# Gated linear attention: a pair's two heads in the partition halves, one tile per direction, and the states made behind both heads' masked products

## The chip, the cores and the metric

The kernel runs on one core of a Trainium2 chip. The metric is the device time of one execution in microseconds (us). The engines named below are TensorE (PE; its weight loads are PEld), VectorE (DVE), ScalarE (ACT), GpSimd (POOL) and SyncE (SP, which issues the DMAs). Each engine works through its own queue in order and waits on semaphores.

## The reference

Two layers over 256 latent tokens and 256 context tokens, width 1024: a SwiGLU half step, a token mixer, a second half step. The mixer has three branches (latent attention, pooling, gated linear attention), each projected, gated and summed. The change is in the third one. It has four heads with a key width of 64 and a value width of 128, in chunks of 64 tokens, one scan forwards and one backwards over context and latent tokens; for each direction:

```
b = jnp.cumsum(ac, axis=3)                       # log decay within a chunk
b_last = b[:, :, :, -1:, :]
q_t, k_t, k_end = qc * exp(b), kc * exp(-b), kc * exp(b_last - b)
A = where(tril, einsum("bhnik,bhnjk->bhnij", q_t, k_t), 0.0)
o_intra = einsum("bhnij,bhnjv->bhniv", A, vc)
dS = einsum("bhnjk,bhnjv->nbhkv", k_end, vc)
decay = exp(b_last)
S_next = decay[..., None] * S + dS               # scan over the chunks
o = o_intra + einsum("bhnik,bhnkv->bhniv", q_t, S)
```

The two directions' outputs are added, normalized per head and token (RMS), and multiplied by a gate.

## The kernel before, in words

The 512 tokens (latent ones first) are the free axis, features are the partitions. Weights come by DMA into raw tiles and are split into a rounded part `whi` (ACT) and a rest `wlo` (DVE, L197); a dense product is three matmuls, at L219, L220 and L221. Most of the kernel is such products.

`mixer` runs generators side by side. In layer 0 `attend` and then `gla` run as one chain; in layer 1, where queries and outputs are the 256 latent tokens only (`n` is 256), they alternate. After each step of a chain, a table of credits (`FILL`) says how much of `filler` is emitted: dense products of other branches whose matmuls (`fill`, `ps`) stand between the steps on TensorE. A list scheduler then fixes each engine's order; what it made of it is shown below.

`gla` takes the heads in two pairs per layer. For a pair, `gla_prepare` makes both directions' logits, decays and sums. `la` is k_end (L1175), turned token-major by transposes (L1189) into `ket`. `qt` and `kt` are q_t and k_t: one tile per head, with direction 0 in partitions 0 to 63 and direction 1 in 64 to 127; since the sources `gq`, `gk` and `e` hold the pair's heads in partition halves, this takes six VectorE instructions of 64 partitions per direction (L1182 to L1184, the last for the decays `dec`).

`gla_pair` then takes one head after the other: 16 small products `ds` (L1210, 64 tokens by 64 key columns, 128 value columns), 14 state steps on VectorE (L1222 and L1224, 64 partitions by 128), the products `A` (L1231), two masked copies (L1232) and their sum `Asum` (L1237); after a step of `filler`, the output `o`: A times values (L1244) and query times state (L1246), where one matmul has both directions in its 128 rows; the first chunk of each direction has a zero state that GpSimd sets (L1212, L1213). Square, sum, Ln, Exp and a product (L1255) normalize it, and it is transposed back (`ot`, L1259).

Of the kernel before, what the change touches and what calls it, by code (L numbers as in the profile page):

```python
# [12 lines left out]
ALU = mybir.AluOpType  # L13
AX = mybir.AxisListType

P = 128
# [121 lines left out]
class Net:  # L138
# [1002 lines left out]
    def gla_prepare(self, c, ready):  # L1141


        nc, l, n = self.nc, self.l, self.n
        cst, vec = self.cst, self.vec[l]
        rst = cst[:, C_RST:C_RST + T]
        gq, gk = self.gq[c], self.gk[c]
        chunk = lambda t: t.rearrange("p (n c) -> p n c", c=64)
# [9 lines left out]
        for d, ps in enumerate(logits):  # L1158
# [20 lines left out]
            o = slice(d * 64, d * 64 + 64)  # L1179
            for hh in range(2):  # L1180
                r = slice(hh * 64, hh * 64 + 64)
                nc.vector.scalar_tensor_tensor(out=qt[hh][o, 0:n], in0=gq[r, 0:n], scalar=0.125, in1=e[r, 0:n], op0=ALU.mult, op1=ALU.mult)  # L1182
                nc.vector.tensor_tensor(out=kt[hh][o, 0:n], in0=gk[r, 0:n], in1=b[r, 0:n], op=ALU.mult)
                nc.vector.tensor_copy(dec[o, hh, :], chunk(e)[r, :, end])  # L1184
# [11 lines left out]
    def gla_pair(self, c, qt, kt, ket, dec):  # L1196

        nc, l, n = self.nc, self.l, self.n
        cst, vec, gv = self.cst, self.vec[l], self.gv
        for hh in range(2):  # L1200
            h = 2 * c + hh
            hv = slice(h * P, (h + 1) * P)

            st = [self.slot(name="st").rearrange("p (n v) -> p n v", n=4) for _ in range(2)]
            dst = [self.ps("ds").rearrange("p (n v) -> p n v", n=4) for _ in range(2)]
            for ch in range(8):
                tt, par = ch // 2, ch % 2
                r = slice(par * 64, par * 64 + 64)
                for d in range(2):
                    nc.tensor.matmul(dst[par][d * 64:d * 64 + 64, tt, :], ket[d][r, tt * P + hh * 64:tt * P + hh * 64 + 64],  # L1210
                                     gv[tt][r, hv], start=True, stop=True)
            nc.gpsimd.memset(st[1][0:64, 0, :], 0.0)  # L1212
            nc.gpsimd.memset(st[1][64:128, 3, :], 0.0)  # L1213
            order = [[4, 5, 6, 7, 0, 1, 2, 3], [7, 6, 5, 4, 3, 2, 1, 0]]
            for i in range(7):
                for d in range(2):
                    o = slice(d * 64, d * 64 + 64)
                    x, y = order[d][i], order[d][i + 1]
                    ds = dst[x % 2][o, x // 2, :]
                    to = st[y // 4][o, y % 4, :]  # L1220
                    if i == 0:
# [168 lines left out]
```

## Time and profile before

| | us |
|---|---|
| Time, median of 3 runs | 2170.09 (2168.61 to 2172.72) |
| Time of the profiled execution | 2169.75 |
| Its span, first to last instruction | 2167.9 |
| TensorE busy | 2081.1 (96% of the span) |
| VectorE busy | 1483.3 (68%) |
| ScalarE busy | 881.2 (41%) |
| Mean granted TensorE clock | 0.984 of full speed |

A busy share is a mean over stages. Matmuls overlap one another in the pipeline, so their durations are longer than the distance from one start to the next; it is the distance that counts for a stretch of them. The time minus the span (1.85 us) is what lies around the profiled instructions.

### The profile page before, as it was taken

To read this page: it belongs to the slowest core of one execution; us is meant where nothing else is said; L and a number is where in the kernel's file an instruction comes from. 1 tells how busy PE (TensorE), PEld (TensorE's weight loads), DVE (VectorE), ACT (ScalarE), POOL (GpSimd) and SP (SyncE) were. 2 spreads that over 40 slices of the span, in tenths; PEclk is the share of its full clock that TensorE was granted. 3 is DMA by queue.
4 is the path that set the end of the run, shared out by engine and by line. 5 is a ranking of instruction groups with operands and counts; after the bars stand their busy time and mean duration, and the time that the engine had idled before them with its cause. 6 is when DMAs were issued, how large, how long until landed. Compare 5 with 4: busy or idle time off the path is not lost.

```text
span 2167.9 us, 29909 instructions
## 1 busy us (share of the span) xinstructions
PE 2081.1 (96%) x11340; PEld 1749.1 (81%) x11340; DVE 1483.3 (68%) x2950; ACT 881.2 (41%) x1797; POOL 5.2 (0%) x26
## 2 busy tenths in 40 slices
PE   7999999898999989999999989999999978999999
PEld 4888878776777778888888888888888867898997
DVE  4577777867686775666876785667554788666564
ACT  5322232445345445433223243223343546565552
POOL 0000000000000000000000000000000000000000
PEclk9999999999999999999999999999999989999999
DMA  9355554514442223445555444456451333466663
GB/s 315 100 157 154 176 166 139 139 55 120 113 112 59 78 65 93 125 121 153 168 169 149 143 138 118 144 145 176 128 139 42 89 90 96 122 172 185 185 194 128
DMA packets 431072, 290.44 MB, mean 134 GB/s; under 512 B 16464, under 2 KB 386768, under 8 KB 430928
## 3 DMA queue, kind: packets, MB, share of 16 engines
q1 hardware_dynamic: 430016, 287.09, 46.0%
q8 instruction: 89, 1.46, 0.3%
q10 hardware_dynamic: 912, 1.44, 0.2%
q14 instruction: 55, 0.45, 0.1%
HBM read 287.44 MB, written 1.05 MB: 133 GB/s over the span
## 4 chain that ended last, share of the span: by engine, by line
PE 72%; DVE 13%; DMA 9%; ACT 4%; issue 2%; ACTq 0%; SPq 0%; DVEq 0%
PE ps L219 17%; PE ps L220 17%; PE ps L221 17%; DMA raw<-in_ffn_w_dram 8%; PE fill L219 4%; DVE wlo L197 4%; PE fill L221 4%; PE fill L220 4%; DVE adaacc L358 2%; ACT whi L185 2%; DVE st L1224 2%; PE sc L1031 1%; PE av L1067 1%; PE pt L1049 1%; PE ada L327 1%
## 5 line engine op out<-in xcount | busy, mean ns | idle before, releaser
L197 DVE TENSOR_TENSOR wlo<-raw,whi 128x512 fp32r<-128x512 f32 (+3 forms) x912 | 531.4, 619 | 290.2 <-ACT whi L185 282.4
L185 ACT ACTIVATE whi<-raw 128x512 fp32r<-128x512 f32 (+3 forms) x912 | 472.2, 568 | 521.7 <-DMA raw<-in_ffn_w_dram 472.5
L219 PE MATMUL ps<-uhi,whi 128*128 128x512 f32 (+1 forms) x1620 | 565.3, 351 | 8.1 <-ACT uhi L185 5.1
L221 PE MATMUL ps<-uhi,wlo 128*128 128x512 f32 (+1 forms) x1620 | 563.2, 348 | 1.0 <-DVE wlo L197 0.9
L220 PE MATMUL ps<-ulo,whi 128*128 128x512 f32 (+1 forms) x1620 | 563.8, 348 | 0.0
L219 PEld LDWEIGHTS ps<-uhi,whi 128*128 128x128 f32 x1620 | 309.1, 192 | 52.7 <-ACT uhi L185 8.3
L221 PEld LDWEIGHTS ps<-uhi,wlo 128*128 128x128 f32 x1620 | 310.1, 191 | 41.0 <-DVE wlo L197 3.0
L220 PEld LDWEIGHTS ps<-ulo,whi 128*128 128x128 f32 x1620 | 310.3, 192 | 38.1 <-DVE ulo L475 0.8
L358 DVE SCALAR_TENSOR_TENSOR adaacc<-raw,csil,adaacc 128x512 f32<-128x512 f32 x420 | 294.6, 744 | 1.0 <-DMA raw<-in_w_ada_dram 0.2
L219 PE MATMUL ps<-hi,whi 128*128 128x512 f32 (+1 forms) x738 | 271.4, 369 | 8.0 <-DVE h L501 6.6
L221 PE MATMUL ps<-hi,wlo 128*128 128x512 f32 (+1 forms) x738 | 270.6, 367 | 0.0
L220 PE MATMUL ps<-lo,whi 128*128 128x512 f32 (+1 forms) x738 | 270.4, 367 | 0.0
L219 PE MATMUL fill<-uhi,whi 128*128 128x512 f32 (+1 forms) x576 | 204.7, 355 | 0.0
L221 PE MATMUL fill<-uhi,wlo 128*128 128x512 f32 (+1 forms) x576 | 196.6, 341 | 0.0
L220 PE MATMUL fill<-ulo,whi 128*128 128x512 f32 (+1 forms) x576 | 196.3, 341 | 0.0
L219 PEld LDWEIGHTS ps<-hi,whi 128*128 128x128 f32 x738 | 139.8, 190 | 30.8 <-DVE h L501 7.0
L221 PEld LDWEIGHTS ps<-hi,wlo 128*128 128x128 f32 x738 | 140.0, 190 | 22.6
L220 PEld LDWEIGHTS ps<-lo,whi 128*128 128x128 f32 x738 | 140.0, 190 | 22.5 <-DVE lo L197 0.2
L570 DVE TENSOR_TENSOR silu<-silu,ps 128x512 f32<-128x512 f32 (+1 forms) x88 | 54.2, 616 | 131.2 <-ACT silu L185 79.9
L219 PEld LDWEIGHTS fill<-uhi,whi 128*128 128x128 f32 x576 | 110.0, 191 | 21.9 <-issue 10.3
L185 ACT ACTIVATE silu<-ps 128x512 f32<-128x512 f32 (+1 forms) x88 | 47.4, 538 | 194.5 <-PE ps L221 194.5
L220 PEld LDWEIGHTS fill<-ulo,whi 128*128 128x128 f32 x576 | 110.1, 191 | 13.7 <-issue 2.6
(267 smaller groups left out, 2215.8 us busy)
## 6 DMA issues: line engine op xcount, KB each, us to landing
raw<-in_ffn_w_dram SPq DMA_DIRECT2D x198, 512.0 KB, 4.4
raw<-in_w_ada_dram SPq DMA_DIRECT2D x128, 512.0 KB, 3.8
raw<-in_w_in_dram SPq DMA_DIRECT2D x86, 512.0 KB, 4.4
raw<-in_ffn_w_dram SPq DMA_DIRECT2D x48, 384.0 KB, 4.1
raw<-in_ffn_w_dram SPq DMA_DIRECT2D x48, 320.0 KB, 3.2
raw<-in_w_branch_dram SPq DMA_DIRECT2D x48, 256.0 KB, 2.8
ada<-in_w_ada_dram SPq DMA_DIRECT2D x32, 256.0 KB, 5.4
raw<-in_w_out_dram SPq DMA_DIRECT2D x16, 512.0 KB, 4.9
```

Of the source, the lines that this page charges most:

```text
L185: i = self.nc.scalar.activation(**k)
L197: self.nc.vector.tensor_tensor(out=lo, in0=src, in1=f32hi, op=ALU.subtract)
L219: mm(out, wh, xh, start=start, stop=False)
L220: mm(out, wh, xl, start=False, stop=False)
L221: mm(out, wl, xh, start=False, stop=stop)
L327: nc.tensor.matmul(ps[32 * g:32 * g + 32, :], self.csil[:, k, :], r[i], start=(k < 4), stop=(k >= 4))
L358: nc.vector.scalar_tensor_tensor(out=acc[s], in0=r[i], scalar=c, in1=acc[s], op0=ALU.mult, op1=ALU.add)
L570: nc.vector.tensor_tensor(out=s[:, 0:n], in0=s[:, 0:n], in1=p3[:, 0:n], op=ALU.mult)
L1031: nc.tensor.matmul(sc[:, 0:nk], q[h][:, tt * P:(tt + 1) * P], keys[h][:, k0:T], start=True, stop=True)
L1049: nc.tensor.transpose(pt[:, (2 * x + j) * P:(2 * x + j + 1) * P], ps_[j][:, (kt + x) * P:(kt + x + 1) * P], self.ident)
L1067: nc.tensor.matmul(av[0][64 * x:64 * x + 64, s * NL:(s + 1) * NL], v[2 * s + kt][:, (h + x) * 64:(h + x) * 64 + 64], pts[x][kt // 2][:, (k ...
L1224: nc.vector.scalar_tensor_tensor(out=to, in0=st[x // 4][o, x % 4, :], scalar=dec[o, hh, x:x + 1], in1=ds, op0=ALU.mult, op1=ALU.add)
```

## The change

`qt`, `kt` and `dec` now have one tile per direction, with the pair's two heads in the partition halves, so three VectorE instructions of 128 partitions per direction make them. `gla_pair` first makes the products A, the masks and the sums of both heads, then, after a step of `filler`, for each direction the `ds` products of both heads (seven chunks, not eight: the last chunk's product was never used) and seven state steps of 128 partitions that serve both heads. The outputs follow head by head: one matmul for each chunk and direction, with 64 rows, without those whose state is zero; the GpSimd memsets are gone. The transposes of both heads come at the end. The number of steps (yields) of the generator is the same, and so is the amount of `filler` between pairs.

```diff
--- before.py
+++ after.py
@@ -1176,12 +1176,9 @@
             ket.append(la)
             self.act(out=e, in_=b, func=AF.Exp, scale=1.0 / 16)
             self.act(out=b[:, 0:n], in_=b[:, 0:n], func=AF.Exp, scale=-1.0 / 16)
-            o = slice(d * 64, d * 64 + 64)
-            for hh in range(2):
-                r = slice(hh * 64, hh * 64 + 64)
-                nc.vector.scalar_tensor_tensor(out=qt[hh][o, 0:n], in0=gq[r, 0:n], scalar=0.125, in1=e[r, 0:n], op0=ALU.mult, op1=ALU.mult)
-                nc.vector.tensor_tensor(out=kt[hh][o, 0:n], in0=gk[r, 0:n], in1=b[r, 0:n], op=ALU.mult)
-                nc.vector.tensor_copy(dec[o, hh, :], chunk(e)[r, :, end])
+            nc.vector.scalar_tensor_tensor(out=qt[d][:, 0:n], in0=gq[:, 0:n], scalar=0.125, in1=e[:, 0:n], op0=ALU.mult, op1=ALU.mult)
+            nc.vector.tensor_tensor(out=kt[d][:, 0:n], in0=gk[:, 0:n], in1=b[:, 0:n], op=ALU.mult)
+            nc.vector.tensor_copy(dec[:, d, :], chunk(e)[:, :, end])
             yield "g1"
         for d in range(2):
             pt = self.ps("ket")
@@ -1197,54 +1194,60 @@
 
         nc, l, n = self.nc, self.l, self.n
         cst, vec, gv = self.cst, self.vec[l], self.gv
+        nt = n // P
+        order = [[4, 5, 6, 7, 0, 1, 2, 3], [7, 6, 5, 4, 3, 2, 1, 0]]
+        hvs = [slice((2 * c + hh) * P, (2 * c + hh + 1) * P) for hh in range(2)]
+        As = []
         for hh in range(2):
-            h = 2 * c + hh
-            hv = slice(h * P, (h + 1) * P)
-
-            st = [self.slot(name="st").rearrange("p (n v) -> p n v", n=4) for _ in range(2)]
-            dst = [self.ps("ds").rearrange("p (n v) -> p n v", n=4) for _ in range(2)]
-            for ch in range(8):
-                tt, par = ch // 2, ch % 2
-                r = slice(par * 64, par * 64 + 64)
-                for d in range(2):
-                    nc.tensor.matmul(dst[par][d * 64:d * 64 + 64, tt, :], ket[d][r, tt * P + hh * 64:tt * P + hh * 64 + 64],
-                                     gv[tt][r, hv], start=True, stop=True)
-            nc.gpsimd.memset(st[1][0:64, 0, :], 0.0)
-            nc.gpsimd.memset(st[1][64:128, 3, :], 0.0)
-            order = [[4, 5, 6, 7, 0, 1, 2, 3], [7, 6, 5, 4, 3, 2, 1, 0]]
-            for i in range(7):
-                for d in range(2):
-                    o = slice(d * 64, d * 64 + 64)
-                    x, y = order[d][i], order[d][i + 1]
-                    ds = dst[x % 2][o, x // 2, :]
-                    to = st[y // 4][o, y % 4, :]
-                    if i == 0:
-                        nc.vector.tensor_copy(to, ds)
-                    else:
-                        nc.vector.scalar_tensor_tensor(out=to, in0=st[x // 4][o, x % 4, :], scalar=dec[o, hh, x:x + 1], in1=ds,
-                                                       op0=ALU.mult, op1=ALU.add)
+            o = slice(hh * 64, hh * 64 + 64)
             for d in range(2):
-                o = slice(d * 64, d * 64 + 64)
                 ps = self.ps("A")
-                for tt in range(n // P):
+                for tt in range(nt):
                     t = slice(tt * P, (tt + 1) * P)
-                    nc.tensor.matmul(ps[:, t], kt[hh][o, t], qt[hh][o, t], start=True, stop=True)
+                    nc.tensor.matmul(ps[:, t], kt[d][o, t], qt[d][o, t], start=True, stop=True)
                 nc.vector.copy_predicated(
                     out=self.amask[d][:, 0:n].rearrange("p (t i) -> p t i", i=P),
-                    mask=self.msk[:, d:d + 1, :].to_broadcast([P, n // P, P]),
+                    mask=self.msk[:, d:d + 1, :].to_broadcast([P, nt, P]),
                     data=ps[:, 0:n].rearrange("p (t i) -> p t i", i=P))
             A = self.slot(name="Asum")
             nc.vector.tensor_tensor(out=A[:, 0:n], in0=self.amask[0][:, 0:n], in1=self.amask[1][:, 0:n], op=ALU.add)
-            yield "g3"
-
+            As.append(A)
+        yield "g3"
+
+        sts = []
+        for d in range(2):
+            st = [self.slot(name="st").rearrange("p (n v) -> p n v", n=4) for _ in range(2)]
+            dst = [self.ps("ds").rearrange("p (n v) -> p n v", n=4) for _ in range(2)]
+            for x in order[d][0:7]:
+                tt, par = divmod(x, 2)
+                r = slice(par * 64, par * 64 + 64)
+                for hh in range(2):
+                    nc.tensor.matmul(dst[par][hh * 64:hh * 64 + 64, tt, :], ket[d][r, tt * P + hh * 64:tt * P + hh * 64 + 64],
+                                     gv[tt][r, hvs[hh]], start=True, stop=True)
+            for i in range(7):
+                x, y = order[d][i], order[d][i + 1]
+                ds, to = dst[x % 2][:, x // 2, :], st[y // 4][:, y % 4, :]
+                if i == 0:
+                    nc.vector.tensor_copy(to, ds)
+                else:
+                    nc.vector.scalar_tensor_tensor(out=to, in0=st[x // 4][:, x % 4, :], scalar=dec[:, d, x:x + 1], in1=ds,
+                                                   op0=ALU.mult, op1=ALU.add)
+            sts.append(st)
+        yield "g3"
+        sqs = []
+        for hh in range(2):
+
+            hv, A, o = hvs[hh], As[hh], slice(hh * 64, hh * 64 + 64)
             po = self.ps("o")
-            nt = n // P
             for tt in range(nt):
                 t = slice(tt * P, (tt + 1) * P)
                 nc.tensor.matmul(po[:, t], A[:, t], gv[tt][:, hv], start=(tt == 0), stop=False)
             for ch in range(2 * nt):
-                nc.tensor.matmul(po[(ch % 2) * 64:(ch % 2) * 64 + 64, (ch // 2) * P:(ch // 2 + 1) * P], qt[hh][:, ch * 64:ch * 64 + 64],
-                                 st[ch // 4][:, ch % 4, :], start=False, stop=(ch >= 2 * nt - 2))
+                for d in range(2):
+                    if ch != order[d][0]:
+                        nc.tensor.matmul(po[(ch % 2) * 64:(ch % 2) * 64 + 64, (ch // 2) * P:(ch // 2 + 1) * P],
+                                         qt[d][o, ch * 64:ch * 64 + 64], sts[d][ch // 4][o, ch % 4, :],
+                                         start=False, stop=(ch >= 2 * nt - 2 and d == (0 if ch == 7 else 1)))
             sq = self.slot(name="sqo")
             self.act(out=sq[:, 0:n], in_=po[:, 0:n], func=AF.Square)
             rstd = self.tiny(8, "orstd")
@@ -1253,7 +1256,9 @@
             self.act(out=rstd[:, 4:4 + nt], in_=rstd[:, 0:nt], func=AF.Ln, scale=1.0 / P, bias=self.eps[:, 0:1])
             self.act(out=rstd[:, 4:4 + nt], in_=rstd[:, 4:4 + nt], func=AF.Exp, scale=-0.5)
             nc.vector.tensor_tensor(out=by_tile(sq), in0=by_tile(po), in1=rstd[:, 4:4 + nt].unsqueeze(2).to_broadcast([P, nt, P]), op=ALU.mult)
+            sqs.append(sq)
             yield "g4"
+        for sq in sqs:
             pt = self.ps("ot")
             for tt in range(nt):
                 nc.tensor.transpose(pt[:, tt * P:(tt + 1) * P], sq[:, tt * P:(tt + 1) * P], self.ident)
```

What it does to the order. On TensorE, layer 0, first pair: before, from the first head's `ds` to its transposes (`ps` and `fill` rows between are left out and counted in the text behind).

```order
L1210 MATMUL ds<-gv,ket 64x128 x16
L1231 MATMUL A<-qt,kt 128x128 x8
L219 MATMUL ps<-hi,whi 128x512
...
L1244 MATMUL o<-gv,Asum 128x128 x4
L1246 MATMUL o<-st,qt 64x128 x8
L219 MATMUL fill<-uhi,whi 128x512
...
L1259 MATMUL ot<-cst_72,sqo 128x128 x4
```

The same engine and place after the change, for both heads.

```order
L1207 MATMUL A<-qt,kt 128x128 x16
...
L1225 MATMUL ds<-gv,ket 64x128 x28
...
L1244 MATMUL o<-gv,Asum 128x128 x4
L1248 MATMUL o<-st,qt 64x128
L219 MATMUL fill<-uhi,whi 128x512
L220 MATMUL fill<-ulo,whi 128x512
L1248 MATMUL o<-st,qt 64x128 x13
...
L1244 MATMUL o<-gv,Asum 128x128 x4
L1248 MATMUL o<-st,qt 64x128 x14
...
L1264 MATMUL ot<-cst_72,sqo 128x128 x8
```

Before, 24 `ps` matmuls stand between A and `o` of the first head and 21 `fill` matmuls for the second. Now 24 `ps` matmuls stand between A and `ds`, and 12 `fill` matmuls between `ds` and the first `o`; 22 more come before the second `o`. In the second pair of layer 0 it was 21 and 9 between A and `o`, and is now 12 between A and `ds`, 24 between `ds` and `o`, and 12 between the two outputs.

On VectorE, the same place, before (one head).

```order
L796 TENSOR_TENSOR gate<-gate 128x512
L1222 COPY st<-ds 64x128 x2
L1224 SCALAR_TENSOR_TENSOR st<-st,dec,ds 64x128 x12
L1232 COPY_PREDICATED amask_181<-msk,A 128x512
L1232 COPY_PREDICATED amask_182<-msk,A 128x512
L794 TENSOR_TENSOR gate<-gate,ps 128x512
L1237 TENSOR_TENSOR Asum<-amask_181,amask_182 128x512
```

And after (both heads; seven rows of dense work, L197, L794 and L796, are left out between).

```order
L1213 TENSOR_TENSOR Asum<-amask_181,amask_182 128x512
L1208 COPY_PREDICATED amask_181<-msk,A 128x512
L1208 COPY_PREDICATED amask_182<-msk,A 128x512
L1213 TENSOR_TENSOR Asum<-amask_181,amask_182 128x512
...
L1231 COPY st<-ds 128x128
L1233 SCALAR_TENSOR_TENSOR st<-st,dec,ds 128x128 x3
L1231 COPY st<-ds 128x128
L1233 SCALAR_TENSOR_TENSOR st<-st,dec,ds 128x128 x8
L197 TENSOR_TENSOR wlo<-raw,whi 128x512
L1233 SCALAR_TENSOR_TENSOR st<-st,dec,ds 128x128
```

The mask sums no longer stand behind the states; the states now end last, and one run of 14 serves both heads where there were two runs.

On TensorE, layer 1, first pair, after the change (`sc` are attention scores, `pool` the pooling branch's product, `rq` a transpose for the attention).

```order
L1225 MATMUL ds<-gv,ket 64x128 x23
L1017 MATMUL rq<-cst_72,rq 128x128 x2
L1031 MATMUL sc<-k,q 128x512 x2
L1244 MATMUL o<-gv,Asum 128x128 x2
L1248 MATMUL o<-st,qt 64x128
L219 MATMUL pool<-hilo,whi 128x256
L1244 MATMUL o<-gv,Asum 128x128 x2
L1248 MATMUL o<-st,qt 64x128
L220 MATMUL pool<-hilo,whi 128x256
L221 MATMUL pool<-hilo,wlo 128x256
L1248 MATMUL o<-st,qt 64x128 x14
```

Before, the first head's `o` stood ahead of `rq` and `sc`, and the second head's `ds`, A and `o` behind them. Now both heads' last 14 output matmuls stand together behind the first scores.

## Rows read from the trace of the kernel before

**Rows 1.** The page's first part: busy time and share of the span, first engines.
```profile
PE 2081.1 (96%) x11340; PEld 1749.1 (81%) x11340; DVE 1483.3 (68%) x2950; ACT 881.2 (41%) x1797; POOL 5.2 (0%) x26
```

**Rows 2.** Windows: us; busy PE, PEld, DVE, ACT, POOL; granted TensorE clock; DMA.
```profile
690.00:820.00 130.00, 119.45 (x725) 95.42 (x724) 95.15 (x176) 65.41 (x114) 1.59 (x8) 0.99 0.24 65
...
1740.00:1790.00 50.00, 36.95 (x266) 28.87 (x265) 42.51 (x114) 23.02 (x58) 0.79 (x4) 0.83 0.40 105
...
1777.00:1784.00 7.00, 7.00 (x38) 6.45 (x39) 5.06 (x13) 4.09 (x10) 0.00 (x0) 0.55 0.21 53
...
1880.00:1920.00 40.00, 40.00 (x335) 39.91 (x334) 26.88 (x54) 26.80 (x58) 0.00 (x0) 1.00 0.70 185
```

**Rows 3.** Timeline of TensorE, layer 0; brackets: idle time before, who ended it.
```profile
729.47 1.16 PE L1244 MATMUL o<-gv,Asum 128*128 128x128 f32 x8 [1.48 <-DVE Asum L1237]
...
744.19 1.13 PE L1244 MATMUL o<-gv,Asum 128*128 128x128 f32 x8 [0.82 <-DVE Asum L1237]
...
770.41 0.66 PE L1189 MATMUL ket<-cst,la 128*128 128x128 f32 x4 [2.60 <-DVE la L1175]
...
790.46 1.13 PE L1244 MATMUL o<-gv,Asum 128*128 128x128 f32 x8 [0.79 <-DVE Asum L1237]
...
805.85 1.13 PE L1244 MATMUL o<-gv,Asum 128*128 128x128 f32 x8 [3.51 <-DVE Asum L1237]
```

**Rows 4.** Timeline of TensorE, layer 1, same columns.
```profile
1758.65 1.19 PE L1244 MATMUL o<-gv,Asum 128*128 128x128 f32 x4 [5.60 <-DVE Asum L1237]
...
1770.98 0.39 PE L219 MATMUL pool<-hilo,whi 128*128 128x256 f32 x1 [2.18 <-ACT hilo L185]
...
1776.82 1.20 PE L1244 MATMUL o<-gv,Asum 128*128 128x128 f32 x4 [2.34 <-DVE Asum L1237]
...
1811.93 1.11 PE L1189 MATMUL ket<-cst,la 128*128 128x128 f32 x4 [5.53 <-DVE la L1175]
...
1827.66 0.68 PE L1244 MATMUL o<-gv,Asum 128*128 128x128 f32 x4 [1.02 <-DVE mx L1035]
...
1849.08 0.71 PE L1244 MATMUL o<-gv,Asum 128*128 128x128 f32 x4 [1.19 <-DVE Asum L1237]
```

**Rows 5.** Timeline of TensorE: shapes of matmuls, each fp32 matmul two records.
```profile
704.85 0.39 PE L219 MATMUL fill<-uhi,whi 128*128 128x512 f32 x1
...
705.08 0.39 PE L220 MATMUL fill<-ulo,whi 128*128 128x512 f32 x1
...
719.56 1.10 PE L1210 MATMUL ds<-gv,ket 64*64 64x128 f32 x32
...
720.60 1.71 PE L1231 MATMUL A<-qt,kt 64*128 64x128 f32 x16
...
730.56 1.09 PE L1246 MATMUL o<-st,qt 128*64 128x128 f32 x16
...
1820.55 0.72 PE L1231 MATMUL A<-qt,kt 64*128 64x128 f32 x8
...
1828.28 0.66 PE L1246 MATMUL o<-st,qt 128*64 128x128 f32 x8
```

**Rows 6.** Timeline of TensorE right after the wait of 3.51 us.
```profile
806.91 1.87 PE L1246 MATMUL o<-st,qt 128*64 128x128 f32 x16
```

**Rows 7.** Groups of VectorE by form: count, busy us, mean ns.
```profile
L1224 DVE SCALAR_TENSOR_TENSOR st<-st,dec,ds 64x128 f32<-64x128 f32 x96 | 33.3, 347 | 3.1
...
L1182 DVE SCALAR_TENSOR_TENSOR qt<-gqk,e 64x512 f32<-64x512 f32 x8 | 5.5, 686 | 0.2
...
L1173 DVE TENSOR_TENSOR la<-b 128x512 f32<-128x512 f32 x8 | 5.5, 690 | 0.2
...
L1182 DVE SCALAR_TENSOR_TENSOR qt<-gqk,e 64x256 f32<-64x256 f32 x8 | 3.4, 420 | 0.2
...
L1184 DVE COPY dec<-e 64x8 f32<-64x8 f32 x16 | 2.6, 160 | 0.0
```

**Rows 8.** Timeline of VectorE: one head's twelve state steps in layer 1.
```profile
1752.85 4.51 DVE L1224 SCALAR_TENSOR_TENSOR st<-st,dec,ds 64x128 f32<-64x128 f32 x12
```

## The prediction

> **What bounds the kernel now.** I read the page's busy shares first, then the windows by stage, then TensorE's timeline in the four stretches of the changed code, then VectorE's groups by form. TensorE is busy for 96% of the span [rows 1], so only two things can move the end: work added to TensorE's queue or taken from it, and time in which TensorE stands still or runs at its lower clock. In the stretch of layer 1 just after the changed code TensorE has no idle time at a granted clock of 1.00 (40.00 of 40.00 us) [rows 2], so what is won ahead of it should reach the end whole. In the changed stretches it does stand still: 130 less 119.45, 10.6 us, in layer 0, and 50 less 36.95, 13.1 us, in layer 1's first pair [rows 2]. In the latter VectorE is busy for 42.51 of 50 us: there VectorE is the bound, and TensorE waits for it. The timeline says for what. In layer 0, `o` waits four times for `Asum` (1.48, 0.82, 0.79, 3.51 us) and `ket` once for `la` (2.60) [rows 3]. In layer 1 `o` waits 5.60, 2.34, 1.02 and 1.19 us, a pooling product 2.18, `ket` 5.53 [rows 4]. After the longer waits the granted clock is down: 0.55 in the mean from 1777 to 1784, so mostly the level of 1.2 GHz [rows 2].
>
> **The change, part by part.**
>
> *VectorE's work.* A state step of 64 partitions by 128 takes 347 ns, and there are 96, with 16 copies ahead of them [rows 7]; twelve in a row take 4.51 us, 0.376 each [rows 8]. The new step has 128 partitions and the same 128 elements. No row shows it, but 64x512 takes 686 ns where 128x512 takes 690 [rows 7], so partitions are free and I take 0.376. The upper bound, cost by partitions, would be 0.75. Per pair 14 steps go: 14 x 0.376 = 5.3 us. In `gla_prepare` one of each two `qt`, `kt` and `dec` goes: four 64-partition products of 0.69 (0.42 in layer 1) and two `dec` of 0.16 [rows 7], so 3.1 us per pair in layer 0 and 2.0 in layer 1. VectorE loses 2 x 8.4 + 2 x 7.3, some 31 us. Where TensorE doesn't wait for it this is worth nothing.
>
> *TensorE's work.* Start to start counts. An fp32 matmul is two records here: 16 `ds` matmuls on four quarters of the array take 1.04 us (719.56 to 720.60), 0.0325 per record. The old state product, 128 rows by 64 columns in two column halves in turn, takes about 1.03 for 16 records, 0.064 each. `A`, 64 rows by 128 columns, takes 1.71 for 16 records and 0.72 for 8 [rows 5]: about 0.10 per record where eight of a row half follow one another, and less where only four do, so some of the second half ran beside the first.
> The new state product has 64 rows of one half and 64 columns, and the column half changes after every two matmuls. Its bounds: 0.064 per record if the column halves always run side by side, 0.13 if they never do (`o` from A, on the whole array, takes 1.13 for 8 records at full clock [rows 3], the last one's tail off). The few records that each half holds are as short a run as the 8-record `A`, which did overlap, so I take 0.07. Layer 0: 28 records x 0.07 = 1.96 for 1.03, four heads, +3.7. Layer 1: 16 x 0.07 = 1.12 for about 0.6 [rows 5], four heads, +2.1. The 28 `ds` instead of 32 save 0.26 per pair, 1.0. In layer 1 `A` now has one row half per head, eight records in a row (8 x 0.10, 0.82, for 0.65, which is the 0.72 without the last record's tail): +0.7. Sum **+5.5 us**; with 0.064 it is +4.4, with 0.13 +16.
>
> A strict order of records is between the two: of the eight records of four matmuls, the second matmul's in a column half hold up those behind them, and only the last of one half runs beside the first of the other. That is six steps for eight records, three quarters of 0.13, some 0.10: +7.1 and +4.0 and the rest, +10.8; a rival below. The Trainium skill states such an order (TensorE: Matmul & The Clock Gate, Part 2): weight loads are pulled ahead, matmuls stay in the program's order. The 16 records of `A` in 1.71 [rows 5] neither show nor exclude it.
>
> *Layer 0, first pair.* Both masks' sums are done under the 24 `ps` matmuls behind A (24 x 0.23 = 5.5 us [rows 5]), so the waits of 1.48 and 0.82 go. A new one comes: the first chunk's output needs the backward scan's last state. That is 5.3 us of steps plus one `wlo` (0.6) after `ds`, and VectorE may be half a microsecond behind: 6.2. TensorE's cover is 12 `fill` (2.7), A times values (1.1) and a few more: 4.3. It waits about 1.8 us, once. **-0.5.**
>
> *Layer 0, second pair.* Ahead of `la` one `qt` less: the wait of 2.60 becomes 1.9, **-0.7**. Between `ds` and `o` now stand 24 `fill`, 5.5 us, and 1.1 of values: the states have the time, and 0.79 and 3.51 go, **-4.3**. The lower clock that followed the wait of 3.51 goes too: the state product took 1.87 instead of 1.09 [rows 5, 6], and the next `fill` some 0.6 in all, **-1.4**. The tail, now with both heads' transposes in one place, moves about 0.6 us of ScalarE's work, and hides 0.5 of it: 0.
>
> *Layer 1, first pair.* Here VectorE is the bound. Waits of 5.60 and 2.34 for the sums go (7.9), and with two units of VectorE's work less the 2.18 should halve (-1.1). In their place TensorE waits for the last state. Between `ds` and it stand 5.3 us of steps and some 2 us of row maxima and pooling that the order puts between, and VectorE is about 2 us behind; TensorE has `rq`, the scores and two products of values against it, about 4. So a wait of 5 us, less a part that pooling fills: I take 4.5. **-4.5** together, bounds -9 (no wait) and 0. A wait of that size still lowers the clock as the 5.60 did; the second lowered stretch, 1777 to 1784, goes: 7 us at 0.55 lose 7 x 0.45 = 3.1, **-3.0**.
>
> *Layer 1, second pair.* Cover for the states is 12 `fill`, transposes of the attention and 24 `fill`, some 5.5 us by half the 128x512 spacing, and the `ds` themselves: 1.02 and 1.19 go, **-2.2**. The 5.53 for `la` stays: VectorE's chain ahead of it loses 0.9 us, but 12 `fill` that stood ahead of the wait stand behind `ket` now. 0.
>
> *At nothing:* the memsets (GpSimd is busy for 5.2 us in all [rows 1], and no row of a wait names it as the releaser), ScalarE's work and the DMAs (the counts are the same, the DMA queue's order is untouched).
>
> Sum: 5.5 - 0.5 - 0.7 - 4.3 - 1.4 - 4.5 - 3.0 - 2.2 = **-11.1 us** on the profiled execution's 2169.75: 2158.7. That execution lies 0.3 us under the median of the runs, 2170.09, so against the median the change is worth 11.4 us, 0.5%.
>
> **The rivals.**
> 1. *The column halves overlap less* in the new state product. In strict order +10.8 instead of +5.5: 2164. Without any overlap +16, of which some 2 hide in the wait of layer 1's first pair: -11.1 + 10.5 - 2, 2167. For it: four matmuls of one row half in a row hardly overlap with the next in `A` (1.71). Against it: the 8-record `A`, 0.72 where 8 records of the whole array take 1.13.
> 2. *The wait moves to the states and grows: slower.* Both heads now wait for one chain that ends with the last state, behind everything that VectorE's order has ahead of it. I put 1.8 us in the first pair and 4.5 in the third. If VectorE is 4 us later in each of the four pairs than I take it, that costs 16 us at full clock, and two more lowered stretches like 1777 to 1784 cost 6: 2169.75 - 11.1 + 22, about 2180. It decides from some 3 us per pair on. For it: VectorE is the bound in the third pair, and its order puts other work between the steps there. Against it: in the second and fourth pair 5.5 us and more cover the chain, and VectorE has 8 us less to do.
> 3. *The gain is larger:* no state wait in layer 1's first pair, so its idle time mostly goes and the clock stays up: -4.5 and -3.0 become -9 and -6, about 2151.
> 4. *The gain doesn't reach the end:* VectorE's saving lies where TensorE has other work, and the state product eats the rest. The waits for `la` (2.60, 5.53) and for attention stay; -11.1 becomes -3: 2167.
>
> **How the numbers follow.** A measurement of this kernel tells about 0.2%, 4.3 us, from no change. My forecast, 2154 to 2162 (own range), has 0.50; rival 1 0.10 in strict order and 0.06 without overlap; rival 2 0.12; rival 3 0.12; rival 4 0.10. Predicted: 2158.7. The range from 2150 to 2168 takes in all but rival 2 and a part of the tails. Faster: 0.50, 0.10 and 0.12, 0.72. Same: 0.06 and 0.10, 0.16. Slower: 0.12.
>
> **What would show it.** VectorE busy down by about 30 us, state steps of 128 partitions at about 350 ns; TensorE's `o` no longer waiting for `Asum`, one wait of 1 to 2 us for a state in layer 0's first pair and none in its second; some 4 to 5 us of waiting in layer 1's first pair, and one lowered stretch less there and one less in layer 0. The 28 records of a state product would take about 2 us. Wrong would be: 0.7 us per step, the state product at 3 us, or longer waits before `o` in all four pairs.

## The result, and the profile after

The changed kernel takes 2154.88 us (median of four runs, 2152.27 to 2158.43), the kernel before, beside it, 2171.40. The ratio is 0.9922, 95% interval 0.9907 to 0.9937: 0.8% faster. A second measurement, where the kernel before took 2164.75, gave 0.9929 (0.9911 to 0.9948). The medians of this section and the next leave out three slow executions (6113.42 us of the changed kernel, 2217.98 and 2584.53 of the kernel before). The forecast was 2158.7. Profiled execution against profiled execution it was -11.1 us; measured were 2152.27 - 2169.75 = -17.5. The profiled execution of the changed kernel is the fastest of its four; between the medians it was 16.5 us.

The page's busy times, to be set against [rows 1]:

```profile
span 2150.5 us, 29894 instructions
...
PE 2084.2 (97%) x11388; PEld 1752.5 (81%) x11388; DVE 1453.7 (68%) x2870; ACT 882.3 (41%) x1797; POOL 2.0 (0%) x10
```

VectorE's busy time fell by 29.6 us, TensorE's rose by 3.1, and the span fell by 17.4. VectorE's groups by form say how the steps were priced (count, busy us, mean ns, idle before):

```profile
L1233 DVE SCALAR_TENSOR_TENSOR st<-st,dec,ds 128x128 f32<-128x128 f32 x48 | 15.2, 343 | 0.7
L1179 DVE SCALAR_TENSOR_TENSOR qt<-gqk,e 128x512 f32<-128x512 f32 x4 | 2.8, 692 | 0.1
```

343 ns with 128 partitions, 347 with 64 [rows 7]: the second head's partitions cost nothing. The windows (span of the row, length, then busy time and count of TensorE, its weight loads, VectorE, ScalarE, GpSimd, then the granted clock) answer to [rows 2]:

```profile
690.00:820.00 130.00, 128.03 (x796) 104.43 (x793) 85.53 (x148) 70.71 (x123) 0.00 (x0) 1.00 0.25 67
...
1740.00:1790.00 50.00, 40.88 (x295) 31.50 (x295) 41.09 (x103) 30.86 (x68) 0.00 (x0) 0.85 0.31 82
1860.00:1900.00 40.00, 40.00 (x335) 39.91 (x334) 25.68 (x50) 26.79 (x59) 0.00 (x0) 1.00 0.76 198
```

In layer 0 TensorE's idle time fell from 10.6 to 2.0 us, at full clock throughout. In layer 1 it is idle for 9.1 of these 50 us, but the changed kernel is ahead here, and 4.1 of them (from 1785.93) already belong to the second pair's wait for `la`, shown below. Over the first pair's own stage in each kernel (1727.33 to 1792.58, now 1719.01 to 1774.44) the idle time fell from 13.1 to 5.3 us. TensorE's timeline in layer 0, against [rows 3, 5] (start, length, what, in brackets the idle time ahead and who ended it):

```profile
733.38 1.05 PE L1244 MATMUL o<-gv,Asum 128*128 128x128 f32 x8
734.36 0.43 PE L1248 MATMUL o<-st,qt 64*64 64x128 f32 x2
735.94 1.75 PE L1248 MATMUL o<-st,qt 64*64 64x128 f32 x26 [0.48 <-DVE st L1233]
742.74 1.05 PE L1244 MATMUL o<-gv,Asum 128*128 128x128 f32 x8
743.72 1.80 PE L1248 MATMUL o<-st,qt 64*64 64x128 f32 x28
745.44 0.50 PE L219 MATMUL fill<-uhi,whi 128*128 128x512 f32 x1
...
766.79 1.03 PE L1186 MATMUL ket<-cst,la 128*128 128x128 f32 x8
```

None of the four waits for `Asum` is left, `ket` doesn't wait for `la` at all, and the new wait for a state is 0.48 us. 28 records of the state product take 745.44 - 743.72 = 1.72 us, 0.061 each. In layer 1, against [rows 4]:

```profile
1734.67 0.66 PE L1186 MATMUL ket<-cst,la 128*128 128x128 f32 x4 [0.20 <-DVE la L1175]
1746.49 0.71 PE L1244 MATMUL o<-gv,Asum 128*128 128x128 f32 x4 [1.67 <-DVE op L1128]
1748.31 0.69 PE L1248 MATMUL o<-st,qt 64*64 64x128 f32 x2 [1.11 <-DVE st L1233]
1750.83 0.58 PE L219 MATMUL pool<-hilo,whi 128*128 128x256 f32 x1 [1.84 <-ACT hilo L185]
...
1794.02 1.11 PE L1186 MATMUL ket<-cst,la 128*128 128x128 f32 x4 [8.09 <-DVE la L1175]
```

The waits of 5.60 and 2.34 us before `o` became 1.67, which the pooling branch's `op` ends, and 1.11, which a state ends; the wait for `la` in the second pair grew from 5.53 to 8.09.

The four stages of the changed code, each from one matmul of the trace to another (first `logit` to first `logit` of the next pair; for layer 0's second pair to the first `ps` behind the last `ot`; for layer 1's second pair to the end of the span), in us:

| kernel (profiled execution) | layer 0, pair 1 | layer 0, pair 2 | layer 1, pair 1 | layer 1, pair 2 to the end | the four together |
|---|---|---|---|---|---|
| before | 56.9 | 67.4 | 65.3 | 375.3 | 564.9 |
| changed | 56.2 | 59.4 | 55.4 | 376.0 | 547.1 |
| changed, again | 56.2 | 59.4 | 55.2 | 374.8 | 545.7 |
| `order_only` | 57.4 | 62.1 | 62.9 | 377.4 | 559.7 |
| `tiles_again` | 55.9 | 59.9 | 56.8 | 372.7 | 545.3 |
| `prep_halves` | 58.2 | 59.5 | 58.5 | 376.6 | 552.8 |
| `steps_halves` | 61.6 | 63.4 | 60.1 | 378.5 | 563.6 |
| `both_halves` | 62.0 | 65.1 | 63.5 | 378.5 | 569.2 |
| `gates_together` | 55.9 | 59.4 | 57.7 | 370.3 | 543.3 |
| `ket_late` | 56.2 | 59.4 | 62.2 | 361.7 | 539.5 |
| `tiles_ket_late` | 55.9 | 59.8 | 63.4 | 365.6 | 544.7 |

Between the two layers the stage is 910.3 us before and after. In the last three kernels layer 1's second `logit` stands elsewhere, so only the sum of the last two stages compares.

### The profile page after: what moved, and what is told of

Same layout as the page of the kernel before. It is cut to its first block, busy times and chain, and to the rows that moved or that the text cites. A ratio compares the mean times of both kernels' runs of the same rounds, so it can differ in the third digit from the quotient of the medians.

```text
span 2150.5 us, 29894 instructions
## 1 busy us (share of the span) xinstructions
PE 2084.2 (97%) x11388; PEld 1752.5 (81%) x11388; DVE 1453.7 (68%) x2870; ACT 882.3 (41%) x1797; POOL 2.0 (0%) x10
## 4 chain that ended last, share of the span: by engine, by line
PE 74%; DVE 11%; DMA 9%; ACT 3%; issue 2%; ACTq 0%; SPq 0%; DVEq 0%
PE ps L219 17%; PE ps L220 17%; PE ps L221 17%; DMA raw<-in_ffn_w_dram 9%; PE fill L219 4%; PE fill L221 4%; PE fill L220 4%; DVE wlo L197 4%; DVE adaacc L358 2%; ACT whi L185 2%; PE sc L1031 1%; PE av L1067 1%; PE ada L327 1%; PE pt L1049 1%; PE gv L219 1%
## 5 line engine op out<-in xcount | busy, mean ns | idle before, releaser
L197 DVE TENSOR_TENSOR wlo<-raw,whi 128x512 fp32r<-128x512 f32 (+3 forms) x912 | 531.3, 619 | 290.0 <-ACT whi L185 279.6
L219 PEld LDWEIGHTS fill<-uhi,whi 128*128 128x128 f32 x576 | 109.3, 190 | 21.7 <-issue 10.6
```

The costliest lines, as they stand in the source:

```text
L197: self.nc.vector.tensor_tensor(out=lo, in0=src, in1=f32hi, op=ALU.subtract)
L219: mm(out, wh, xh, start=start, stop=False)
```

## The experiments

Two accounts stood against each other. **W:** TensorE gains because VectorE has less to do where TensorE waits for it (14 steps instead of 28 per pair, one `qt`, `kt` and `dec` instead of two). **O:** it gains because of the order (both masked sums first, the states behind them, filler as cover). The prediction had used both. The kernel before took 2163.4 to 2164.8 us beside the experiments, some 5 less than where their expectations start from, so the ratios are to be compared, each against the kernel before, with its interval (`tiles_only` and `tiles_again` are one kernel):

| kernel | median us | ratio to before |
|---|---|---|
| `order_only` | 2158.75 | 0.9971 (0.9957 to 0.9985) |
| `tiles_only` | 2147.94 | 0.9922 (0.9904 to 0.9940) |
| `tiles_again` | 2147.59 | 0.9921 (0.9903 to 0.9940) |
| `after_again` (the changed kernel) | 2148.22 | 0.9929 (0.9911 to 0.9948) |
| `prep_halves` | 2155.88 | 0.9963 (0.9949 to 0.9978) |
| `steps_halves` | 2166.39 | 1.0012 (1.0000 to 1.0023) |
| `both_halves` | 2172.53 | 1.0038 (1.0023 to 1.0052) |
| `tiles_fill` | 2150.98 | 0.9939 (0.9922 to 0.9956) |
| `gates_together` | 2145.07 | 0.9910 (0.9894 to 0.9926) |
| `gates_tiles` | 2146.12 | 0.9914 (0.9898 to 0.9929) |
| `ket_late` | 2143.17 | 0.9893 (0.9875 to 0.9912) |
| `tiles_ket_late` | 2146.55 | 0.9921 (0.9907 to 0.9934) |

**The order alone, the tiles alone.** `order_only` keeps before's tiles and steps:

```diff
+        for hh in range(2):          # A, masks, sum of both heads
+            ...
+            As.append(A)
+        yield "g3"
+        for hh in range(2):          # 16 ds and 14 steps of 64 partitions per head
+            ...
+            sts.append(st)
+        yield "g3"
+        for hh in range(2):          # o of both heads; then the transposes of both
```

> Before's tiles (a tile per head, steps of 64 partitions, two state tiles zeroed in a corner), but the changed order: both heads' masked sums, then both heads' states, then both outputs, then the transposes. Theory W (the gain is VectorE's smaller work where TensorE waits for it): VectorE stays at about 1483 us, the wait of 2.60 us for `la` in layer 0's second pair stays, 28 steps of 64 partitions stand behind the masks, and `o` waits 4 to 5 us for a state in each layer's first pair: 2167 to 2172 us, no gain. Theory O (the gain is the order, masks first and states behind with filler as their cover): the waits for `Asum` go all the same, 2155 to 2162 us.

`tiles_only` has the changed tiles in before's order, but for the states, which serve both heads and so come first:

```diff
+        # ds and states of the pair, as in the changed kernel, come first, without a yield
         for hh in range(2):
             ...
-            As.append(A)
-        yield "g3"
+            yield "g3"               # then o of this head, g4, its transposes, g5
```

> The changed tiles (a tile per direction, steps of 128 partitions, the state product of 28 records), but before's order: states of the pair, then for each head A, mask, sum, output, transpose. Theory W: VectorE at about 1454 us, the wait for `la` in layer 0's second pair gone as after the change; 2153 to 2159 us. Theory O: `o` waits for `Asum` four times in each layer as before, 3.5 us and 5.6 us the longest, and the state product costs 3 to 5 us more; 2165 to 2172 us.

The order alone gave 0.3%. Set against 2170 us, where the expectations start from, O asked for 0.4 to 0.7%, W for nothing: it lies between. The tiles alone gave 0.8%, all that the change gave. They don't add up, since both take the waits for `Asum` out of layer 0. TensorE's four first output products of layer 0 in `tiles_only`, none with idle time ahead:

```profile
723.19 1.05 PE L1237 MATMUL o<-gv,Asum 128*128 128x128 f32 x8
...
737.05 1.05 PE L1237 MATMUL o<-gv,Asum 128*128 128x128 f32 x8
...
779.36 1.05 PE L1237 MATMUL o<-gv,Asum 128*128 128x128 f32 x8
...
792.82 1.05 PE L1237 MATMUL o<-gv,Asum 128*128 128x128 f32 x8
```

What the order left standing, in TensorE's timeline of `order_only`:

```profile
730.78 1.09 PE L1255 MATMUL o<-st,qt 128*64 128x128 f32 x16 [2.24 <-DVE st L1242]
...
765.57 0.66 PE L1189 MATMUL ket<-cst,la 128*128 128x128 f32 x4 [2.61 <-DVE la L1175]
...
1751.96 0.68 PE L1253 MATMUL o<-gv,Asum 128*128 128x128 f32 x4 [3.58 <-DVE st L1242]
...
1758.33 0.58 PE L219 MATMUL pool<-hilo,whi 128*128 128x256 f32 x1 [4.77 <-ACT hilo L185]
...
1799.35 1.12 PE L1189 MATMUL ket<-cst,la 128*128 128x128 f32 x4 [8.34 <-DVE la L1175]
```

28 steps behind the masks make `o` wait for a state, and `pool` waits longer in layer 1's first pair. The tiles, timed again beside the changed kernel:

> The changed kernel itself, timed again beside the next three on one chip: about 0.992 of before. Its wait of `ket` for `la` in layer 1's second pair is 8.1 us.

> The new tiles in before's order, timed beside the changed kernel. If the new order is worth something on top of the tiles, this kernel is 3 us or more slower than the changed one. If the order only takes away waits that the tiles take away too, and puts 12 `fill` products behind the wait for `la` in layer 1's second pair, it is equal in layer 0 and 2 to 4 us faster in all: 0.990 to 0.991 of before.

The two can't be told apart (0.9921 and 0.9929, overlapping intervals). Layer 0 is equal, and the trace agrees with the account of layer 1's second pair; in `tiles_again`:

```profile
1738.83 0.71 PE L1237 MATMUL o<-gv,Asum 128*128 128x128 f32 x4 [1.88 <-DVE Asum L1231]
...
1752.54 0.38 PE L219 MATMUL pool<-hilo,whi 128*128 128x256 f32 x1 [2.60 <-ACT hilo L185]
...
1790.02 1.12 PE L1186 MATMUL ket<-cst,la 128*128 128x128 f32 x4 [5.91 <-DVE la L1175]
```

The wait for `la` is 5.91 here, as before the change, and 8.34 in `order_only`: its growth comes with the order. But the 2 to 4 us that I expected from it didn't show in the time. By the stages the second pair is 2.1 us shorter than in `after_again` and the first 1.6 longer: in the main the 12 `fill` (1.4 us) change places.

**The halves put back.** Two edits of the changed kernel undo VectorE's saving without touching the order, and a third does both:

```diff
-            nc.vector.scalar_tensor_tensor(out=qt[d][:, 0:n], ...)   # kt and dec likewise
+            for hh in range(2):
+                r = slice(hh * 64, hh * 64 + 64)
+                nc.vector.scalar_tensor_tensor(out=qt[d][r, 0:n], ...)
...
-                ds, to = dst[x % 2][:, x // 2, :], st[y // 4][:, y % 4, :]
+                for hh in range(2):
+                    r = slice(hh * 64, hh * 64 + 64)
+                    ds, to = dst[x % 2][r, x // 2, :], st[y // 4][r, y % 4, :]
```

> The changed kernel, with `qt`, `kt` and `dec` each made by two instructions on 64 partitions instead of one on 128. VectorE +10 us busy. Theory W: the wait of `ket` for `la` in layer 0's second pair is back at 2 to 2.6 us, in layer 1 the 8.09 us grows by about 1 and the first pair's waits by about 1: 2157 to 2160 us, 3 to 5 us over the changed kernel. Theory O: within 1.5 us of the changed kernel's 2154.9.

> The changed kernel, with each state copy and step in two instructions on 64 partitions instead of one on 128: 28 per pair instead of 14, VectorE +19 us busy. Theory W: `o` waits for the state 5 us longer in each layer's first pair (0.48 becomes 5 to 6, 1.11 becomes 6), nothing in layer 0's second pair: +8 to +10 us, 2163 to 2165 us. Theory O: the filler behind the masks covers the steps: within 3 us of the changed kernel, under 2158 us.

> The changed kernel with `qt`, `kt`, `dec` and every state step in two instructions of 64 partitions: VectorE's busy time of before (1484 us) with the new tiles and the new order. If the gain is VectorE's smaller work, the costs of the two parts (6 us and 17 us by the stages of their runs) add up: 20 to 24 us over the changed kernel, so 3 to 7 us slower than before. If they fall into the same waits, 15 to 18 us over the changed kernel, about before's time. If the arrangement itself (release of tiles, order) carried the gain, under 10 us over the changed kernel.

Against `after_again` the first costs 7.7 us by the medians, the second 18.2, both together 24.3 (7.7 + 18.2 = 25.9). That is W, and more of it than expected: with VectorE's old amount of work (1484.5 us busy) the new arrangement is 0.4% slower than before, while before's tiles in the same order are 0.3% faster. So without the saving the changed kernel has no gain left, and the saving pays for the longer state product too. This is shown in the new order; no run has the halves put back in before's order. `steps_halves` shows the sizes. TensorE in layer 0's two pairs and in layer 1's first:

```profile
737.27 2.75 PE L1250 MATMUL o<-st,qt 64*64 64x128 f32 x26 [2.68 <-DVE st L1235]
...
797.79 1.87 PE L1250 MATMUL o<-st,qt 64*64 64x128 f32 x26 [1.81 <-DVE st L1235]
...
1762.82 1.97 PE L1250 MATMUL o<-st,qt 64*64 64x128 f32 x14 [6.74 <-DVE st L1235]
```

and VectorE in layer 0's second pair, ahead of the second of these waits:

```profile
787.78 0.61 DVE L1233 COPY st<-ds 64x128 f32<-64x128 f32 x2 [0.60 <-PE ds L1225]
788.42 4.52 DVE L1235 SCALAR_TENSOR_TENSOR st<-st,dec,ds 64x128 f32<-64x128 f32 x12
792.97 0.61 DVE L1233 COPY st<-ds 64x128 f32<-64x128 f32 x2
793.61 4.51 DVE L1235 SCALAR_TENSOR_TENSOR st<-st,dec,ds 64x128 f32<-64x128 f32 x12
```

The chain of 28 takes 798.12 - 787.78 = 10.3 us, more than the filler between `ds` and `o` covers even in the second pair, where I had expected no wait. In the changed kernel the same place reads:

```profile
786.18 0.29 DVE L1231 COPY st<-ds 128x128 f32<-128x128 f32 x1 [0.61 <-PE ds L1225]
786.51 1.50 DVE L1233 SCALAR_TENSOR_TENSOR st<-st,dec,ds 128x128 f32<-128x128 f32 x4
787.92 0.28 DVE L1231 COPY st<-ds 128x128 f32<-128x128 f32 x1
788.12 2.64 DVE L1233 SCALAR_TENSOR_TENSOR st<-st,dec,ds 128x128 f32<-128x128 f32 x8
```

14 steps in 790.76 - 786.18 = 4.6 us. Behind the wait of 2.68 us the clock fell; the window of `steps_halves` has a mean of 0.72:

```profile
735.00:747.00 12.00, 9.73 (x71) 8.24 (x71) 5.87 (x12) 2.63 (x6) 0.00 (x0) 0.72 0.26 72
```

The cost of `prep_halves` is not where its expectation put it. Two rows of its TensorE carry most of it:

```profile
732.37 1.75 PE L1250 MATMUL o<-st,qt 64*64 64x128 f32 x26 [0.90 <-DVE st L1235]
...
1735.29 0.65 PE L1188 MATMUL ket<-cst,la 128*128 128x128 f32 x4 [1.67 <-DVE la L1175]
```

In layer 0's first pair the wait for a state is only 0.4 us longer, but the granted clock behind it is down (0.84 from 731.5 to 742) and the stage takes 2.0 us more. In layer 1's first pair `ket` waits 1.67 us where it waited 0.20, and the stage takes 3 us more. The wait for `la` in layer 1's second pair, expected to grow by about 1 us, is 8.18.

Another term went against W: in `prep_halves` layer 0's wait for `la` did not come back (its second pair takes 59.5 us, as in the changed kernel), although VectorE makes `qt` in halves as before: `ket` starts at 764.80 without idle time ahead. ScalarE's timeline tells why. `order_only`, then `prep_halves`, where the second direction's gate chain begins (`e<-logit`); their second `logit` starts at 744.85 and 747.28:

```profile
753.97 0.60 ACT L185 ACTIVATE gate<-fill 128x512 f32<-128x512 f32 x1 [0.88 <-DVE qt L1182]
754.57 1.15 ACT L185 ACTIVATE whi<-raw 128x512 fp32r<-128x512 f32 x2
757.12 0.69 ACT L185 ACTIVATE e<-logit,vec 128x512 f32<-128x512 f32 x1 [1.40 <-PE fill L221]
```

```profile
756.87 0.63 ACT L185 ACTIVATE whi<-raw 128x512 fp32r<-128x512 f32 x1 [0.41 <-DVE dec L1183]
757.41 0.67 ACT L185 ACTIVATE e<-logit,vec 128x512 f32<-128x512 f32 x1
```

With a tile per head, ScalarE's `gate` waits for head 1's `qt` and `e` for a `fill`, and `e` starts 12.27 us after `logit`; with a tile per direction 10.13. Neither is an input of what waits, so I read these as waits for a tile's memory to come free; that is argued from the names in the rows. What is shown is that the smaller number of instructions was not the cause, so these 2.6 us are not W's.

**The wait for `la` in layer 1.** Since the changed kernel stands still for 8 us there, three edits tried to cover it: more filler ahead (`tiles_fill`, the layer 1 credit `g1` from 0.5 to 2), both directions' chains written together (`gates_together`, and `gates_tiles` on before's order), `ket` one step of attention later (`ket_late`, and `tiles_ket_late`).

```diff
             nc.vector.tensor_copy(dec[:, d, :], chunk(e)[:, :, end])
-            yield "g1"
+        for _ in range(2):          # gates_together
+            yield "g1"
...
             yield "g1"
+        if not self.full:           # ket_late: layer 1 only
+            yield "g2"
         for d in range(2):
             pt = self.ps("ket")
```

> The new tiles in before's order, with 2 instead of 0.5 as layer 1's filler credit for a direction's gate chain (`g1`), so that more `ps` products of the projection stand ahead of the wait for `la`. If TensorE's 5.9 us in front of `ket` in layer 1's second pair is only for lack of work, it falls by 2 to 4 us and the kernel gains as much against the one without. If the products are missed later, as cover in front of `o`, waits of the same size come back there and the time is the same within 2 us.

It missed. In the second pair 48 `fill` products stand behind `logit` and ahead of this `ket` instead of 24, some 2.9 us, but `la` came later by as much (`ket` starts 22.1 us after `logit` instead of 19.2), and the wait stayed. In the first pair a `pool` product waits 4.74 us instead of 2.60. The time is 3.4 us longer by the medians, the intervals overlapping. That is nearest to the expectation's second case, with the wait coming back in front of `pool` and not of `o`.

```profile
1795.87 1.11 PE L1186 MATMUL ket<-cst,la 128*128 128x128 f32 x4 [6.26 <-DVE la L1175]
```

> The changed kernel, with the gate chains of both directions written one behind the other, and the two points at which attention and filler go on behind them. TensorE's order in the second pairs is the same. If the 8.1 us that `ket` waits for `la` in layer 1's second pair stand for the second direction's chain, which starts 10 us after the first because attention's row maxima, gates and weight halves stand between, the wait falls to 2 to 5 us and the kernel is 3 to 8 us faster than the changed one (0.989 to 0.991 of before). If VectorE and ScalarE just have that much to do before it, it stays at 7 to 8 us and the time within 2 us.

> The same edit of the gate chains on the new tiles in before's order. Its wait for `la` is 5.9 us without the edit. If the second direction's chain is what is late, the wait falls to 1 to 3 us and the kernel is 2 to 6 us faster than without; if VectorE's work ahead of it is the bound, it is the same within 2 us.

The chains written together brought the wait from 8.09 to 2.27 us, as the first account said:

```profile
1786.91 0.66 PE L1187 MATMUL ket<-cst,la 128*128 128x128 f32 x4 [2.27 <-DVE la L1175]
1788.45 1.97 PE L1049 MATMUL pt<-cst,p 128*128 128x128 f32 x8 [0.88 <-DVE gate L794]
```

The second direction's chain had simply begun late: its `e` now starts 6.9 us after the second pair's `logit`, in the changed kernel 12.7. The time gained (0.9929 to 0.9910) is 3 us by the medians, within the overlap of the intervals. On before's order the same edit took the wait in front of `ket` from 5.91 to 1.67 us, now ended by a `gate`, as expected, but gave 1.5 us instead of 2 to 6, no difference that can be measured.

> The changed kernel, with the transposes of `ket` one step of attention later in layer 1: 24 or 36 products of 128x256, `pt` and `av` stand between `logit` and `ket` that stood behind. If TensorE's wait for `la` is only a matter of what stands ahead of it in its queue, it goes (8.1 becomes under 2 us, less `pt` waiting for its `p`), and the kernel is 4 to 8 us faster than the changed one unless the products are missed in front of `o`. If VectorE is the bound of this stretch, TensorE waits for `p` or a state instead, 5 to 8 us in all, and the time stays within 2 us.

> The later `ket` of layer 1 on the new tiles in before's order, where head 1's masked sum stands behind head 0's output. With the wait for `la` gone in both, what is left tells what the new order is worth by itself: if it is worth nothing, this kernel lies at 0.988 to 0.991 of before, as the one with the new order (0.9893); if the order of masks and states matters once `ket` no longer waits, this one waits for `Asum` or a state by 3 us or more in layer 1 and lies at 0.991 to 0.993.

`ket_late` has the lowest median of the study: 0.9893 of before, 5.0 us under the changed kernel, the intervals touching at 0.9911 to 0.9912 (and overlapping with the first measurement of the change, 0.9907 to 0.9937). Its wait for `la` is gone; `o` waits for a state in its place, less long:

```profile
1752.32 0.43 PE L1250 MATMUL o<-st,qt 64*64 64x128 f32 x2 [0.57 <-DVE st L1235]
...
1756.38 1.97 PE L1250 MATMUL o<-st,qt 64*64 64x128 f32 x14 [3.63 <-DVE st L1235]
```

With before's order the edit is worth nothing (0.9921, as without it): `ot` now waits for the normalized output. In `tiles_ket_late`:

```profile
1752.45 0.69 PE L1257 MATMUL ot<-cst,sqo 128*128 128x128 f32 x2 [3.19 <-DVE sqo L1253]
...
1821.58 0.44 PE L1257 MATMUL ot<-cst,sqo 128*128 128x128 f32 x2 [1.92 <-DVE sqo L1253]
```

So the order is worth something after all once `ket` no longer waits, 3.4 us by the medians and 5.2 by the stages; the intervals (0.9875 to 0.9912 and 0.9907 to 0.9934) overlap a little, so this is likely, not settled.

## Why the prediction was right, step by step

The forecast (faster, by 0.5%) has the right sign and, in the main, the right mechanism: less work on VectorE, fewer waits of TensorE, a state product that costs a few microseconds more. The size was too small by 6 us on the profiled execution, 5 between the medians (16.5 against 11.4). Term by term:

- **TensorE's work, +5.5:** +4.2. By starts, 28 records of the state product take 1.72 us instead of 1.02 (four heads, +2.8), 16 in layer 1 1.07 instead of 0.59 (+1.9); 56 `ds` 1.69 instead of twice 1.03 (four pairs, -1.5); `A` in layer 1 +0.7, as forecast, in layer 0 +0.3. The value taken between the bounds, 0.07 per record, measured 0.061, just under the lower bound, and 0.067. On the whole array 8 records take 743.72 - 742.74 = 0.98 us, 0.12 each, so the column halves run side by side, and rival 1 falls in both forms: strict order had given 0.10. The Trainium skill states that matmuls stay in program order (TensorE: Matmul & The Clock Gate, Part 2); the trace doesn't tell whether this rule or my working of it fails.
- **Layer 0, first pair, -0.5 for waits:** -1.8. The new wait was put at 1.8 us and measured 0.48: I had the 14 steps at 5.3 us; they took 4.6 in the second pair's rows, where a step that follows one of the other direction starts 0.26 us behind it (788.12, 788.38, 788.64) and one that follows its own 0.38. (The parts of that estimate, 5.3, 0.6 and 0.5, add up to 6.4 and not 6.2, so the wait should have been 2.1.) With TensorE's +1.2 the stage moved by -0.7.
- **Layer 0, second pair:** -4.3 for `Asum` is as forecast, and the lower clock after it is gone (1.00 in the window). The wait for `la`, put at -0.7, gave -2.6: its step, "one `qt` less", named the wrong cause, as `prep_halves` shows. The stage moved by -7.9.
- **Layer 1, first pair, -4.5 and -3.0:** -9.8 for the stage, about -6.3 forecast with TensorE's part. `o` waits 1.67 + 1.11 where I took 4.5, and only the 1.11 is for a state; `ket` waits 0.20 for 1.78, which the forecast left out (`prep_halves` puts it back at 1.67, so this one is VectorE's saving). The `pool` waits did not halve: 1.84 and a later 0.44 for 2.18. The lowered clock shrank less than forecast: the mean over the stage is 0.88 for 0.87, so by my estimate 0.12 x 55.4 = 6.7 us are lost instead of 0.13 x 65.3 = 8.5, 1.8 less and not 3.0. And some 1.4 us is no gain: 12 `fill` of 128x256, 0.12 each, moved behind the second `logit`.
- **Layer 1, second pair, -2.2 and the 5.53 as before:** the waits of 1.02 and 1.19 are gone, but the 5.53 became 8.09. I had seen both sides, 0.9 us less on VectorE against 12 `fill` less ahead of `ket`, and let them cancel. The time from `logit` to the `ket` that waits for `la` did not shrink (19.4 us before, 19.6 after), because the second direction starts late, not because it is long. The longer wait also costs clock: 0.52 from 1789 to 1799. With TensorE's part and the moved `fill` the stage stayed as it was (+0.7, in the second trace -0.5).

One sentence of the reasoning fell. The prediction explained the end of the waits for `Asum` by the new order; `tiles_only` has before's order and none of them in layer 0. The tiles would have done it alone. Rival 2 (the wait moves to the states and grows) is what `steps_halves` made of the kernel: it decides at 28 steps per pair, not at 14. Rival 3 (2151) lies as near to the median of 2154.88 as the forecast (2158.7), and nearer to the 2152.27 of the profiled execution, from which both were worked out. But the state wait that it left out is there, at 1.11 us, and part of the gain comes from terms that neither had right (the wait for `la` in layer 0, `ket`'s 1.78). Rival 4 is true of one wait only: the 5.53 for `la` stayed and grew.

## What to carry to other kernels

Where an engine on the path waits for a chain of small VectorE instructions, put independent work into the free partitions: both heads in one instruction cost 343 ns where one cost 347, and undoing that took the whole gain away. A new order and fewer instructions can remove the same wait, so measure each alone before giving credit to both. When a wait grows elsewhere, ask when the chain waited for starts, not only how long it is: asking for its result one step later lowered the median by another 0.2% here, at the edge of what these runs can tell.

## What the runs showed that was not expected

- Row halves overlap by their order. 32 records of `A` took 3.42 us when 16 of one half followed 16 of the other, and 2.75 in `order_only`, where the half changes after every 8 (both by starts).
- 28 records of 64 rows by 64 columns, the column half changing every four, take 0.061 us each; before's 16 with 128 rows, the half changing every two, 0.064. Per record, half the rows cost nothing and save nothing.
- A wait of 0.48 us in layer 0's first pair left the clock at 1.00, one of 2.68 in the same place (`steps_halves`) was followed by a mean of 0.72 over 12 us, and one of 0.90 (`prep_halves`) by 0.84 over 10.5. The length of the wait alone doesn't tell: before's wait of 1.48 us there [rows 3] left 1.00 over the whole pair. The lowered clock is where putting the halves back cost more than the waits.
